# Wider PSUM adds and a new order of the first loads in a windowed matmul

## The chip, the cores and the metric

One core of one Trainium2 chip. The metric is the device time of one execution in microseconds (us). Kernels of one batch ran on the same chip, in turn with the kernel before; the last batch alone shares seven of its eight times of the kernel before with the first, which ran on the same chip. Engines in the profile: PE (matmuls), PEld (weight loads), DVE (VectorE), ACT (ScalarE), POOL (GpSimd), SP (SyncE); a name with q, as in SPq, is that engine's sequencer, which issues the DMAs. The granted clock, for short the clock, is the share of PE's full clock that PE was given in a stretch: 1.00 is all of it.

## The reference

```python
# x: (4, 4096, 4096) float32, w: (4096, 4096) float32, offsets: (4,) int64
for b in range(4):
    o = int(offsets[b])
    results.append(x[b, o:o+64] @ w)
return np.stack(results)          # (4, 64, 4096) float32
```

Four windows of 64 rows make 256 rows, so the work is a 256 x 4096 by 4096 x 4096 product. `w` is 67 MB in float32 and has to be read once; it is by far the most of the traffic.

## The kernel before

The 256 rows are two groups `g` of 128. The 4096 output columns are eight pieces of 512, one PSUM bank each. Pool's DMAs load `w` and cast it to fp16 on the way. Only the first k tile (`w0_32`, 128 rows of `w`) is loaded in float32 on the two hardware queues, one half each, and cast by ScalarE. The windows' offsets are a tiny load of four numbers, which Pool has to read before it can issue the four loads of x.

```python
blocks = [(0,1),(1,1),(2,4),(6,4),(10,4),(14,4),(18,4),(22,3),(25,2),(27,1)]   # first k tile, how many
n_join = 2;  k_tail = 28;  n_fine = 2
tmp = [acc_pool.tile([P, NT], fp32, name=f"tmp{i}") for i in range(4)]
ps  = [psum_pool.tile([P, NT], fp32, name=f"bank{t}") for t in range(8)]       # eight tiles of a bank

nc.sync.dma_start(out=w0_32[:, :NG], in_=w[0:P, :NG])
nc.scalar.dma_start(out=off_t[:], in_=offsets[None, :])
nc.scalar.dma_start(out=w0_32[:, NG:], in_=w[0:P, NG:])
...                                   # cut: casts, second k tile, x loads, weight stream, transposes
def add_out(bank, g, c):
    dst = acc[g][:, c * NT : (c + 1) * NT]
    nc.vector.tensor_add(out=dst, in0=dst, in1=ps[bank][:])

def whole_rows(kts, cols, first):     # stream: block by block, all columns
    for g in range(G):
        for c in cols:
            bank = n_bank % 8; n_bank += 1
            for i, kt in enumerate(kts):
                mm(bank, g, kt, ...)
            if not first: add_out(bank, g, c)
            ...                       # cut: the first block copies in place of adding

def columns(ng, kts):                 # column stages: k outside, four banks per g
    for ki in kts:
        for g in range(G):
            for j in range(n_sub): tail_mm(ki, g, ng, j, ...)     # bank 4 * g + j
    for g in range(G):
        for j in range(0, n_sub, 2):
            add_out(4 * g + j, g, ng * n_sub + j)
            nc.scalar.copy(out=tmp[2 * g + j // 2][:], in_=ps[4 * g + j + 1][:])
    ...                               # cut: the adds from tmp
...                                   # cut: two column stages, stores, k tiles 28 and 29
for h in range(2):                    # the end: two halves of the last two k tiles
    js = range(h * n_sub // 2, (h + 1) * n_sub // 2)
    for ki in range(k_fine, n_k):
        for g in range(G):
            for j in js: tail_mm(ki, g, ng, j, ...)
    for g in range(G):
        for j in js: add_out(4 * g + j, g, ng * n_sub + j)
        store(q[g], g, ...)
```

The last tiles are taken by column stages so that finished halves of the output can be stored while the rest is computed.

Of the kernel before, what the change touches and what calls it, by code (L numbers as in the profile page):

```python
# [10 lines left out]
def kernel(  # L11
# [7 lines left out]
    nc = tc.nc  # L19
    fp32 = mybir.dt.float32  # L20
# [5 lines left out]
    P = 128  # L26
    NT = 512
    NG = N // 2
    n_k = D // P
    n_sub = NG // NT  # L30
    G = B // 2
# [13 lines left out]
    acc_pool = ctx.enter_context(tc.tile_pool(name="acc", bufs=1))  # L45
    psum_pool = ctx.enter_context(tc.tile_pool(name="ps", bufs=1, space=bass.MemoryType.PSUM))

    identity = const_pool.tile([P, P], fp16, name="identity")
    off_t = const_pool.tile([1, B], mybir.dt.int64, name="off_t")
    x16 = [x_pool.tile([P, D], fp16, name=f"xrow{g}") for g in range(G)]  # L50
    xT = [x_pool.tile([P, D], fp16, name=f"xT{g}") for g in range(G)]
    w_one = [w1_pool.tile([P, N], fp16, name=f"w1_{i}") for i in range(2)]
    tmp = [acc_pool.tile([P, NT], fp32, name=f"tmp{i}") for i in range(4)]
    acc = [acc_pool.tile([P, N], fp32, name=f"acc{g}") for g in range(G)]
    ps = [psum_pool.tile([P, NT], fp32, name=f"bank{t}") for t in range(8)]

    ctx.enter_context(tc.manual_schedule())

    w0_32 = acc[1]
    nc.sync.dma_start(out=w0_32[:, :NG], in_=w[0:P, :NG])  # L60
    nc.scalar.dma_start(out=off_t[:], in_=offsets[None, :])
    nc.scalar.dma_start(out=w0_32[:, NG:], in_=w[0:P, NG:])
    nc.scalar.copy(out=w_one[0][:, :NG], in_=w0_32[:, :NG])  # L63
    nc.scalar.copy(out=w_one[0][:, NG:], in_=w0_32[:, NG:])  # L64
    off_i32 = off_t.bitcast(mybir.dt.int32)
# [3 lines left out]
    for b in range(B):  # L69
        g, m = divmod(b, 2)  # L70
# [8 lines left out]
            out=x16[g][m * WIN : (m + 1) * WIN, :],  # L79
            in_=x[b][bass.ds(o, WIN), :],  # L80
# [3 lines left out]
    src = {  # L84
        0: lambda a, e: w_one[0][:, a:e],
        1: lambda a, e: w_one[1][:, a:e],
    }
    free = 0
    for k0, r in blocks[2:]:
        if free < r:  # L90
            t = wc_pool.tile([P, R_MAX * N], fp16, name="wc", tag="wc")
# [4 lines left out]
            out=t[:, base : base + r * N],  # L96
            in_=w[k0 * P : (k0 + r) * P, :].rearrange("(p r) n -> p (r n)", r=r),
# [11 lines left out]
    t = wc_pool.tile([P, R_MAX * N], fp16, name="wc", tag="wc")  # L109
    pos = 0  # L110
    for ng, st in zip(order, (steps, fine_steps)):
        for ki, n, c0, c1 in st:
            wd = c1 - c0
            nc.gpsimd.dma_start(  # L114
                out=t[:, pos : pos + n * wd].rearrange("p (t n) -> p t n", t=n),
                in_=w[ki * P : (ki + n) * P, ng * NG + c0 : ng * NG + c1].rearrange(
                    "(t p) n -> p t n", p=P
                ),
# [7 lines left out]
    def x_cols(g, kt):  # L126
        for k0, r in blocks:
            if k0 <= kt < k0 + r:
                a = k0 * P + kt - k0
                return x16[g][:, a : a + r * (P - 1) + 1 : r]  # L130
        return x16[g][:, kt * P : (kt + 1) * P]

    for g in range(G):
        for t in range(8):
            for i in range(4):
                nc.tensor.matmul(  # L136
                    out=ps[t][:, i * P : (i + 1) * P],
                    lhsT=x_cols(g, 4 * t + i),
                    rhs=identity[:],
                    start=True,  # L140
                    stop=True,
                )
            dst = xT[g][:, t * NT : (t + 1) * NT]
            if t % 2 == 0:
                nc.vector.tensor_copy(out=dst, in_=ps[t][:])  # L145
            else:
                nc.scalar.copy(out=dst, in_=ps[t][:])  # L147

    def mm(bank, g, kt, rhs, start, stop):
        nc.tensor.matmul(  # L150
            out=ps[bank][:],
            lhsT=xT[g][:, kt * P : (kt + 1) * P],
            rhs=rhs,
            start=start,
            stop=stop,
        )

    def add_out(bank, g, c):
        dst = acc[g][:, c * NT : (c + 1) * NT]
        nc.vector.tensor_add(out=dst, in0=dst, in1=ps[bank][:])  # L160

    n_bank = 0

    def whole_rows(kts, cols, first):
        nonlocal n_bank
        for g in range(G):
            for c in cols:
                bank = n_bank % 8
                n_bank += 1
                for i, kt in enumerate(kts):  # L170
                    mm(bank, g, kt, src[kt](c * NT, (c + 1) * NT), i == 0, i == len(kts) - 1)
                if not first:
                    add_out(bank, g, c)
                elif c % 2 == 0:
                    nc.vector.tensor_copy(out=acc[g][:, c * NT : (c + 1) * NT], in_=ps[bank][:])  # L175
                else:
                    nc.scalar.copy(out=acc[g][:, c * NT : (c + 1) * NT], in_=ps[bank][:])  # L177

    whole_rows([0, 1], range(8), True)
    for k0, r in blocks[2:-n_join]:  # L180
        whole_rows(range(k0, k0 + r), range(8), False)
    join = range(blocks[-n_join][0], k_tail)

    def tail_mm(ki, g, ng, j, start, stop):
        c = ng * n_sub + j
        rhs = src[ki](c * NT, (c + 1) * NT) if ki < k_tail else tail[(ki, c)]
        mm(4 * g + j, g, ki, rhs, start, stop)
# [3 lines left out]
    def store(eng, g, c0, c1, cuts=(0, P)):  # L191
        for a, e in zip(cuts, cuts[1:]):
            eng.dma_start(out=out_rows[g * P + a : g * P + e, c0:c1], in_=acc[g][a:e, c0:c1])  # L193

    def columns(ng, kts):
        for ki in kts:
            for g in range(G):
                for j in range(n_sub):
                    tail_mm(ki, g, ng, j, ki == kts[0], ki == kts[-1])
        for g in range(G):  # L200
            for j in range(0, n_sub, 2):
                add_out(4 * g + j, g, ng * n_sub + j)
                nc.scalar.copy(out=tmp[2 * g + j // 2][:], in_=ps[4 * g + j + 1][:])  # L203
        for g in range(G):
            for j in range(1, n_sub, 2):
                c = ng * n_sub + j
                dst = acc[g][:, c * NT : (c + 1) * NT]
                nc.vector.tensor_add(out=dst, in0=dst, in1=tmp[2 * g + j // 2][:])  # L208

    columns(order[1], list(join))  # L210
    ng = order[0]
    columns(ng, list(join) + list(range(k_tail, n_k)))
    for g in range(G):
        store(nc.gpsimd, g, ng * NG, (ng + 1) * NG)

    ng = order[1]
# [6 lines left out]
    for h in range(2):  # L223
# [3 lines that stand above are left out]
                for j in js:  # L227
                    tail_mm(ki, g, ng, j, False, ki == n_k - 1)
        for g in range(G):
            for j in js:  # L230
                add_out(4 * g + j, g, ng * n_sub + j)
            c0 = ng * NG + h * NG // 2
            store(q[g], g, c0, c0 + NG // 2)

# [29 lines left out]
```

## Time and profile before

| what | value |
|---|---|
| time, median of 3 | 182.1 us (182.09 to 182.39) |
| span of the profiled run | 180.2 us |
| PE busy | 127.2 us (71%) in 576 instructions |
| DVE busy | 90.6 us (50%) in 136 instructions |
| ACT, POOL busy | 18.3 and 12.7 us |
| read from and written to memory | 71.30 and 4.19 MB |

Busy shares are averages over stages with different limits: neither PE nor DVE is full.

### The profile page before, as it was taken

To read this page: it belongs to the slowest core of one execution; us is meant where nothing else is said; L and a number is where in the kernel's file an instruction comes from. 1 tells how busy PE (TensorE), PEld (TensorE's weight loads), DVE (VectorE), ACT (ScalarE), POOL (GpSimd) and SP (SyncE) were. 2 spreads that over 40 slices of the span, in tenths; PEclk is the share of its full clock that TensorE was granted. 3 is DMA by queue.
4 is the path that set the end of the run, shared out by engine and by line. 5 is a ranking of instruction groups with operands and counts; after the bars stand their busy time and mean duration, and the time that the engine had idled before them with its cause. 6 is when DMAs were issued, how large, how long until landed. Compare 5 with 4: busy or idle time off the path is not lost.

```text
span 180.2 us, 1537 instructions
## 1 busy us (share of the span) xinstructions
PE 127.2 (71%) x576; PEld 57.0 (32%) x576; DVE 90.6 (50%) x136; ACT 18.3 (10%) x27; POOL 12.7 (7%) x27
## 2 busy tenths in 40 slices
PE   0000789104999499938996599949999999998900
PEld 0000754001344134403442134414444444443400
DVE  0000678100487347833686147725879966409560
ACT  2412556200000000000000000000000004004000
POOL 4600000000000100010001000020007100001100
PEclk9999999855699979996999569987999999999995
DMA  5999989999998899999989999989999999999995
GB/s 186 316 256 216 276 175 204 236 233 226 233 226 189 175 233 233 235 222 233 196 189 211 233 233 218 229 180 213 224 209 215 195 211 213 216 211 208 372 411 209
DMA packets 4152, 40.98 MB, mean 227 GB/s; under 512 B 434, under 2 KB 434, under 8 KB 2226
## 3 DMA queue, kind: packets, MB, share of 16 engines
q0 software_dynamic: 3280, 36.70, 93.4%
q1 hardware_dynamic: 432, 2.10, 3.2%
q10 hardware_dynamic: 434, 2.10, 2.9%
q8 instruction: 4, 0.07, 0.1%
q14 instruction: 2, 0.02, 0.0%
HBM read 71.30 MB, written 4.19 MB: 419 GB/s over the span
## 4 chain that ended last, share of the span: by engine, by line
DMA 58%; PE 30%; issue 3%; DVE 2%; another core or an unknown queue 1%; POOL 1%; POOLq 1%; DVEq 0%
DMA wc<-in_w_dram 58%; PE bank L150 30%; DVE acc L160 2%; POOL wc L114 1%; POOLq L71 1%; POOL xrow L78 0%; DVEq L259 0%; POOL identity masks.py:197 0%; POOLq L78 0%; POOL w L67 0%; POOLq masks.py:199 0%; POOLq L248 0%
## 5 line engine op out<-in xcount | busy, mean ns | idle before, releaser
L150 PE MATMUL bank<-wc,xT 128*128 128x512 f16 x480 | 115.0, 405 | 24.3 <-DMA wc<-in_w_dram 24.3
L160 DVE TENSOR_TENSOR acc<-acc,bank 128x512 f32<-128x512 f32 x112 | 75.2, 687 | 61.5 <-PE bank L150 60.9
L150 PEld LDWEIGHTS <-xT 128*128 128x128 f16 x512 | 52.1, 103 | 93.8 <-DMA wc<-in_w_dram 27.2
L136 PE MATMUL bank<-identity,xrow 128*128 128x128 f16 x64 | 5.3, 258 | 20.0 <-DMA xrow<-in_x_dram 20.0
L203 ACT COPY tmp<-bank 128x512 f32<-128x512 f32 x8 | 4.1, 599 | 127.5 <-PE bank L150 127.5
L145 DVE CAST xT<-bank 128x512 f16<-128x512 f32 x8 | 5.3, 687 | 21.0 <-PE bank L136 20.9
L95 POOL DMA_DIRECT2D wc<-in_w_dram x8 | 4.3, 540 | 108.1 <-PE bank L150 108.1
L136 PEld LDWEIGHTS <-xrow 128*128 128x128 f16 x64 | 5.0, 124 | 20.1 <-issue 20.1
L150 PE MATMUL bank<-w,xT 128*128 128x512 f16 x32 | 7.1, 379 | 0.0
L175 DVE COPY acc<-bank 128x512 f32<-128x512 f32 x8 | 5.4, 688 | 0.9 <-PE bank L150 0.6
L114 POOL DMA_DIRECT2D wc<-in_w_dram x6 | 3.9, 674 | 17.1 <-PE bank L150 17.1
L147 ACT CAST xT<-bank 128x512 f16<-128x512 f32 x8 | 4.4, 593 | 7.1 <-PE bank L136 7.0
L208 DVE TENSOR_TENSOR acc<-acc,tmp 128x512 f32<-128x512 f32 x8 | 5.0, 682 | 0.0
L177 ACT COPY acc<-bank 128x512 f32<-128x512 f32 x8 | 4.7, 586 | 2.1 <-PE bank L150 1.9
L193 POOL DMA_DIRECT2D out_dram<-acc x2 | 1.1, 538 | 26.6 <-DVE acc L208 26.6
L64 ACT CAST w<-acc 128x2048 f16<-128x2048 f32 x1 | 1.9, 1897 | 4.9 <-DMA acc<-in_w_dram 4.9
L78 POOL DMA_DIRECT2D xrow<-in_x_dram x4 | 2.1, 524 | 2.1 <-issue 2.1
L63 ACT CAST w<-acc 128x2048 f16<-128x2048 f32 x1 | 1.9, 1897 | 2.8 <-DMA acc<-in_w_dram 2.8
L63 ACT ACT_TABLE_LOAD x1 | 1.3, 1283 | 1.8 <-PEq L248 1.8
L67 POOL DMA_DIRECT2D w<-in_w_dram x1 | 0.7, 660 | 0.8 <-POOLq L248 0.8
masks.py:199 POOL TENSOR_SCALAR_AFFINE_SELECT identity<-identity 128x128 f16<-128x128 f16 x1 | 0.3, 290 | 0.1
masks.py:197 POOL MEMSET identity<- 128x128 f16 x1 | 0.2, 224 | 0.0
(4 smaller groups left out, 0.4 us busy)
## 6 DMA issues: line engine op xcount, KB each, us to landing
wc<-in_w_dram POOLq DMA_DIRECT2D x5, 4096.0 KB, 42.1
wc<-in_w_dram POOLq DMA_DIRECT2D x4, 1024.0 KB, 24.6
wc<-in_w_dram POOLq DMA_DIRECT2D x1, 3072.0 KB, 37.1
xrow<-in_x_dram POOLq DMA_DIRECT2D x4, 512.0 KB, 14.5
wc<-in_w_dram POOLq DMA_DIRECT2D x1, 2048.0 KB, 26.6
out_dram<-acc POOLq DMA_DIRECT2D x2, 1024.0 KB, 6.3
acc<-in_w_dram SPq DMA_DIRECT2D x1, 1024.0 KB, 5.1
w<-in_w_dram POOLq DMA_DIRECT2D x1, 1024.0 KB, 12.0
```

The source lines that it names most:

```text
L63: nc.scalar.copy(out=w_one[0][:, :NG], in_=w0_32[:, :NG])
L95: nc.gpsimd.dma_start(out=t[:, base : base + r * N], in_=w[k0 * P : (k0 + r) * P, :].rearrange("(p r) n -> p (r n)", r=r),)
L114: nc.gpsimd.dma_start(out=t[:, pos : pos + n * wd].rearrange("p (t n) -> p t n", t=n), in_=w[ki * P : (ki + n) * P, ng * NG + c0 : ng * NG ...
L136: nc.tensor.matmul(out=ps[t][:, i * P : (i + 1) * P], lhsT=x_cols(g, 4 * t + i), rhs=identity[:], start=True, stop=True,)
L145: nc.vector.tensor_copy(out=dst, in_=ps[t][:])
L147: nc.scalar.copy(out=dst, in_=ps[t][:])
L150: nc.tensor.matmul(out=ps[bank][:], lhsT=xT[g][:, kt * P : (kt + 1) * P], rhs=rhs, start=start, stop=stop,)
L160: nc.vector.tensor_add(out=dst, in0=dst, in1=ps[bank][:])
L175: nc.vector.tensor_copy(out=acc[g][:, c * NT : (c + 1) * NT], in_=ps[bank][:])
L177: nc.scalar.copy(out=acc[g][:, c * NT : (c + 1) * NT], in_=ps[bank][:])
L203: nc.scalar.copy(out=tmp[2 * g + j // 2][:], in_=ps[4 * g + j + 1][:])
L208: nc.vector.tensor_add(out=dst, in0=dst, in1=tmp[2 * g + j // 2][:])
```

## The change

The intent: fewer and wider DVE instructions, as each add has a fixed part (0.687 us for 512 columns, but 2.288 and not 2.75 for four times as many in the result), and a start in which ScalarE's queue does not hold its half of the first k tile back behind the offsets. PSUM becomes two tiles of four banks ("quads"), the adds of the stream take four banks at once, those of the stages and of the end two, and ScalarE copies two banks at once into a wider `tmp`. The diff, cut to its core:

```diff
-    tmp = [acc_pool.tile([P, NT], fp32, name=f"tmp{i}") for i in range(4)]
+    tmp = [acc_pool.tile([P, 2 * NT], fp32, name=f"tmp{i}") for i in range(G)]
-    ps = [psum_pool.tile([P, NT], fp32, name=f"bank{t}") for t in range(8)]
+    quads = [psum_pool.tile([P, 4 * NT], fp32, name=f"banks{t}") for t in range(2)]
+    def banks(b, n=1):
+        return quads[b // 4][:, b % 4 * NT : (b % 4 + n) * NT]
     nc.sync.dma_start(out=w0_32[:, :NG], in_=w[0:P, :NG])
-    nc.scalar.dma_start(out=off_t[:], in_=offsets[None, :])
     nc.scalar.dma_start(out=w0_32[:, NG:], in_=w[0:P, NG:])
+    nc.sync.dma_start(out=off_t[:], in_=offsets[None, :])
 ... (ps[b][:] becomes banks(b) everywhere)
     whole_rows:
-            for c in cols:
-                bank = n_bank % 8
+            for c in range(0, 2 * n_sub, 4):
+                b0 = n_quad % 2 * 4
+                for j in range(4): (the four banks' matmuls)
-                    add_out(bank, g, c)
+                    add_out(b0, 4, g, c)
     columns:
-            for j in range(0, n_sub, 2):
-                add_out(4 * g + j, g, ng * n_sub + j)
-                nc.scalar.copy(out=tmp[2 * g + j // 2][:], in_=ps[4 * g + j + 1][:])
+            add_out(4 * g, 2, g, ng * n_sub)
+            nc.scalar.copy(out=tmp[g][:], in_=banks(4 * g + 2, 2))
     the end:
-            for j in js:
-                add_out(4 * g + j, g, ng * n_sub + j)
+            add_out(4 * g + js[0], 2, g, ng * n_sub + js[0])
```

## The prediction

> **What bounds the kernel now.** I read the page first: span 180.2 us for a measured 182.1, so 1.9 us lie outside the span and I carry them over. Then the chain, the rows of the groups, and the timelines of the start and of the last 60 us.
>
> ```profile
> DMA  5999989999998899999989999989999999999995
> ...
> DMA 58%; PE 30%; issue 3%; DVE 2%; another core or an unknown queue 1%; POOL 1%; POOLq 1%; DVEq 0%
> ...
> L150 PE MATMUL bank<-wc,xT 128*128 128x512 f16 x480 | 115.0, 405 | 24.3 <-DMA wc<-in_w_dram 24.3
> L160 DVE TENSOR_TENSOR acc<-acc,bank 128x512 f32<-128x512 f32 x112 | 75.2, 687 | 61.5 <-PE bank L150 60.9
> ...
> L203 ACT COPY tmp<-bank 128x512 f32<-128x512 f32 x8 | 4.1, 599 | 127.5 <-PE bank L150 127.5
> ```
>
> The DMA row is full from about 2 us to the end, and PE's idle time (24.3 us) is all waiting for weights. So the weight stream sets the pace. In the timeline the four-tile blocks begin at 43.1, 62.4, 81.7, 101.1 and 120.4 us: 19.35 us apart, against 15.6 to 16.7 us of matmuls. In that stretch PE has 2.6 to 3.8 us to spare per block and DVE waits for PE. Shorter adds there buy nothing.
>
> The end is different. PE alone, from 120 us:
>
> ```profile
> 120.43 43.22 PE L150 MATMUL bank<-wc,xT 128*128 128x512 f16 x192 [2.61 <-DMA wc<-in_w_dram]
> 164.42 0.82 PE L150 MATMUL bank<-wc,xT 128*128 128x512 f16 x3 [0.77 <-DMA wc<-in_w_dram]
> ```
>
> 192 matmuls run without a gap (192 x 0.216 = 41.5, plus 1.7 while the clock is low), then only 0.77 us are spare. PE delayed by more than 0.77 us in this stretch moves everything after it. The end of the chain and the stores:
>
> ```profile
> 164.42 5.37 PE bank L150 x24
> 169.79 1.57 DVE acc L160 x3
> 171.36 0.19 issue
> 171.55 0.69 DVEq L259
> 172.24 1.79 DVE acc L160 x3
> ```
> ```profile
> 166.15 0.54 POOL L193 DMA_DIRECT2D out_dram<-acc  x1 [25.91 <-DVE acc L208]
> 167.35 0.53 POOL L193 DMA_DIRECT2D out_dram<-acc  x1 [0.66 <-DVE acc L208]
> 169.16 4.87 DVE L160 TENSOR_TENSOR acc<-acc,bank 128x512 f32<-128x512 f32 x8 [2.10 <-PE bank L150]
> ```
>
> The last add ends at 174.03, the last store goes out then and lands 5.2 us later, queued behind other stores. And the start:
>
> ```profile
> 0.86 0.52 ACTq L61 DMA_DIRECT2D off_t<-in_offsets_dram  x1
> 0.87 0.38 SPq L60 DMA_DIRECT2D acc<-in_w_dram  x1
> 1.38 0.66 POOL L67 DMA_DIRECT2D w<-in_w_dram  x1 [0.81 <-POOLq L248]
> 1.41 0.38 ACTq L62 DMA_DIRECT2D acc<-in_w_dram  x1
> ...
> 3.54 0.53 POOL L78 DMA_DIRECT2D xrow<-in_x_dram  x1 [0.92 <-issue]
> ```
>
> The offsets are first on their queue and do not delay Pool: it issues its first x load at 3.54. The queue view for 1.5 to 4.5 us shows how the halves of w0 share the engines:
>
> ```profile
> q1 hardware_dynamic: 101, 0.83, 86.0%
> q10 hardware_dynamic: 2, 0.00, 0.0%
> ```
>
> q1 is sync, q10 scalar. Scalar's half, issued at 1.41, has moved nothing at 4.5 us (its two packets are the offsets); the packet records show it beginning at 4.9, when sync's half is ending, and Pool's first weights at 5.4. The scalar half's cast starts only at 12.7, against 5.94 for sync's half.
>
> **What the Trainium skill says.** "VectorE: DVE Perf Modes", section "The TRN2 errata": an fp32 tensor_tensor takes (N+151)/0.96 ns, a fixed part per instruction. The trace agrees: 691 by the formula, 687 measured. So estimates: 1024 columns 1.22 us, 2048 columns 2.29 us. "PSUM — Partial Sum Buffer", section "PSUM bank collisions raise a hardware error": two engines must keep apart per bank; different banks are free. So the chip needs no wait between banks 0 and 1; any such wait in the new program is the program's own. "DMA: Bandwidth & Descriptors", section "Issuing engines are not separate DMA queues": DMAs of different issuers run on the same engines and interleave. Only half seen here: scalar's half did not interleave with sync's, it followed it. "TensorE: Matmul & The Clock Gate", section "What's actually happening": the clock is granted by windows of 3.4 us. The trace fits: after gaps of 2.6 to 3.8 us PE gets 0.5 for a while, after 0.77 us it does not.
>
> **The change part by part.**
>
> Adds of four banks: 96 adds of 0.687 become 24 of 2.29, DVE busy 66 to 55 us, 11 us less. All beside the weight stream: worth 0. Their price: a quad of four banks is one tile, and the built program's waits show that it is handed over whole. PE may write no bank of a quad before the whole add has ended, where it used to get back bank after bank. With two quads this is free while PE needs over 2.3 us a quad: 16 matmuls are 3.46 us, 12 are 2.59. It is not free where the loop form changes.
>
> (A) From the three-tile block to the first column stage: PE needs the second quad 4 matmuls (0.86 us) after its last one, the add takes 0.1 + 2.29 + 0.1 (handing over, my guess from 0.03 to 0.11 between PE's end and an add's start in the timeline). Stall 2.49 - 0.86 = 1.63 us; before, none.
>
> (B) Between the column stages: the program's waits are now add, then scalar's copy of the other two banks, then PE; before, add and copy used separate banks side by side. A 1024-column copy is 599 + 512 x 0.845 = 1.03 us (slope from 599 ns at 512 and 1897 ns at 2048). For g = 0: the quad ends 0.86 us before the stage's end T; add to T+0.46, copy to T+1.59, PE at T+1.69. For g = 1: copy from T+1.76 to T+2.79, PE at T+2.89, wanted at T+2.55. Stall 1.69 + 0.34 = 2.03 us.
>
> (C) The same from the second column stage to the last steps: 2.03 us.
>
> (D) The last half's matmuls now wait for the first half's add in the same quad. With H the end of the first half: add g0 to H+0.89, PE at H+0.99; add g1 to H+2.09, PE at H+2.19; PE ends at H+3.49 and the last add at H+5.55. Before: H = 169.79, last add 174.03, H+4.24. So 1.3 us more; the adds of two banks themselves save next to nothing (four of 1.22 for eight at a pitch of 0.61).
>
> Sum at the last add: 1.63 + 2.03 + 2.03 - 0.77 + 1.3 = 6.2 us, so 180.25. Then the stores. Before they queued; the last packets left at 178.9, 4.9 us after the last add. Now Pool's stores go out some 4 us later, DMA idles after the weights, and the last 512 KB find an empty queue: about 1.0 us to the first packet (0.87 to 1.87 at the start), 1.3 us at 410 GB/s, some 0.6 us of ramp: 183.1. That is 4.2 us later, about 2 us of the delay having been queueing. The tail costs +4.2.
>
> The start: transposes and first copies now take turns within a quad, about 8 us per g (eight turns of some 0.25 us of matmuls, a cast of 0.69 or 0.59 and two handings over, one turn overlapped) for 3.3 and 2.0 before, but PE stood idle from 32.2 to 43.1 us: hidden. The scalar half moves 0.55 us up; sync's half alone already fills the engines (86% share with the ramp), so this buys 0 to 0.4 us. The offsets are now third among hardware-queue loads. If these are served in turn as above, the second half shares the engines with Pool until about 12 us (12.7 in the trace), the offsets land then, and x goes out 1.2 us later (offsets in at about 2.3, first x load 3.54) plus at least 1 us to its first packet. The 4.2 MB of w0 and w1 are through at about 12.3 us, nothing else is queued, and DMA idles some 2.5 us, which shift the whole stream. If the halves and Pool interleave evenly, the offsets land at about 9.5: 0.3 us. If the offsets need only follow sync's half: -0.2 us. With chances 0.55, 0.25 and 0.20 the mean is +1.4.
>
> **The rivals.** (1) DMA bound throughout, so nothing shows: 182. For it the full DMA row; against it the 0.77 us spare. (2) Cheaper adds release banks earlier and the tail shortens: 181 to 182. Against it the whole-quad waits. (3) Only the tail pays: 186.2. (4) Tail and late offsets: 188.7. (5) A stall of 1.7 to 2 us late on also drops PE's clock for a window, up to 1.7 us more; gaps of 2.6 us did, so I give it one chance in three, +0.5.
>
> **Range and chances.** 182.1 + 4.2 + 1.4 + 0.5 = 188.2; I say 188.0, with 185.3 (tail smaller by 1, no bubble) to 190.8 (bubble and a clock drop). The limit of 2% is 185.7. The tail alone passes it by 0.6, so slower 0.84, within 2% 0.14, faster 0.02.
>
> **What would show it.** Adds of 2.29 and 1.22 us, DVE busy near 79 us. PE in the 192-matmul stretch: gaps of about 1.6 and 2.0 us, released by DVE and by scalar's copy. After the weights a hole in the DMA row of 2 to 3 us, the last add about 6 us later against the weights' landing. The first x load at 13 us (4), 11 or 6.5; the block at 43.1 us later by the bubble. I am wrong if the quads' waits are handed over faster than counted, if stores in an empty queue take much less than 2.9 us, or if PE gains slack before 120 us that I don't see.

## The result, and the profile after

The changed kernel took 189.0 us (median of six runs, 187.5 to 190.0), against 182.1 us (182.0 to 182.4) for the kernel before in the same rounds. The ratio is 1.0376, with a 95% interval from 1.0331 to 1.0422: slower by 3.8%. Ratios here and below are the mean time of one kernel's runs over that of the other's runs in the same rounds, so not quite the ratio of the medians quoted. Executions over 1.5% slower than the fastest of the same kernel are left out of the means. The profiled run of the changed kernel took 188.7 us, with a span of 186.9.

From the page of the changed kernel: the busy times, the granted clock and the DMA share in 40 slices of 4.7 us.

```profile
PE 128.3 (69%) x576; PEld 57.9 (31%) x576; DVE 79.1 (42%) x46; ACT 17.5 (9%) x17; POOL 12.7 (7%) x27
...
PEclk9999999999999999996699889999999999999997
DMA  5978999998999999999999998999999999996696
```

The DVE saving came in full: 90 instructions and 11.5 us less. It bought nothing, for the DMA row has two dents that the row of before does not have: one in the third slice (9 to 14 us) and one three to four slices from the end (168 to 178 us). Loads or stores stand still there, and the two dents belong to the two parts of the change. The adds' groups, split by shape:

```profile
L164 DVE TENSOR_TENSOR acc<-acc,banks 128x2048 f32<-128x2048 f32 x24 | 54.9, 2288 | 46.8 <-PE banks L154 46.8
L164 DVE TENSOR_TENSOR acc<-acc,banks 128x1024 f32<-128x1024 f32 x8 | 9.4, 1217 | 17.0 <-PE banks L154 17.0
```

**The start.** The timeline of the changed kernel's start (start, duration, who, what, and in brackets the idle time before and what ended it):

```profile
0.86 0.40 ACTq L65 DMA_DIRECT2D acc<-in_w_dram  x1
0.87 0.38 SPq L64 DMA_DIRECT2D acc<-in_w_dram  x1
...
1.31 0.32 SPq L66 DMA_DIRECT2D off_t<-in_offsets_dram  x1
...
13.11 0.53 POOL L82 DMA_DIRECT2D xrow<-in_x_dram  x1 [10.49 <-issue]
```

The offsets are issued at 1.31 us, but the packet records show their one packet at 10.94, after both halves of `w0` (done at 9.7 and 10.0). Pool reads the offsets at 11.89 and issues the first x load at 13.11, where it was 3.54. The view of the queues between 1.5 and 4.5 us (packets, MB, share of the 16 engines; q1 is sync's, q10 scalar's) shows that the halves now share the engines:

```profile
q1 hardware_dynamic: 49, 0.40, 51.3%
q10 hardware_dynamic: 40, 0.33, 30.5%
```

By the time that x is issued, everything queued ahead of it has run out. In the table of windows (stretch, its length, then busy time of PE, PEld, DVE, ACT and POOL with their instructions, the clock, the DMA share and GB/s), first the changed kernel, then the kernel before:

```profile
13.00:14.00 1.00, 0.00 (x0) 0.00 (x0) 0.00 (x0) 1.00 (x1) 0.53 (x1) 1.00 0.00 0
173.00:174.50 1.50, 1.39 (x7) 0.58 (x6) 1.45 (x2) 0.18 (x1) 0.54 (x1) 1.00 0.00 0
```

```profile
13.00:14.00 1.00, 0.00 (x0) 0.00 (x0) 0.00 (x0) 1.00 (x1) 0.00 (x0) 1.00 0.94 197
62.00:64.00 2.00, 1.63 (x4) 0.58 (x5) 0.00 (x0) 0.00 (x0) 0.00 (x0) 0.57 1.22 262
173.00:174.50 1.50, 0.00 (x0) 0.00 (x0) 1.03 (x2) 0.00 (x0) 0.00 (x0) 1.00 1.05 429
```

DMA stands still from 13.1 to 14.3 us and is thin around it; the last packet of x ends at 26.6 us instead of 22.7. At 173 us it stands still again: all weights are in, and no store is ready. (The line for 62 us is used below, for the clock.)

**The end.** PE of the changed kernel from the 120-us block on:

```profile
124.70 13.99 PE L154 MATMUL banks<-wc,xT 128*128 128x512 f16 x64 [3.63 <-DMA wc<-in_w_dram]
139.16 11.40 PE L154 MATMUL banks<-wc,xT 128*128 128x512 f16 x52 [0.47 <-DMA wc<-in_w_dram]
152.07 4.48 PE L154 MATMUL banks<-wc,xT 128*128 128x512 f16 x20 [1.52 <-DVE acc L164]
158.04 12.51 PE L154 MATMUL banks<-wc,xT 128*128 128x512 f16 x56 [1.49 <-ACT tmp L208]
172.10 5.61 PE L154 MATMUL banks<-wc,xT 128*128 128x512 f16 x24 [1.55 <-ACT tmp L208]
178.59 0.59 PE L154 MATMUL banks<-wc,xT 128*128 128x512 f16 x2 [0.88 <-DVE acc L164]
179.72 1.46 PE L154 MATMUL banks<-wc,xT 128*128 128x512 f16 x6 [0.54 <-DVE acc L164]
```

Where 192 matmuls ran without a gap before, there is now one wait of 0.47 us for weights and then a gap at each change of stage, and the engine that ends each is named: DVE's wide add, then ScalarE's copy twice, then DVE between the two last halves. After 139.16 PE never again waits for weights. From 139.16 to the end of the first half at 172.10 + 5.61 = 177.71 us are 38.55 us for 52 + 20 + 56 + 24 = 152 matmuls, which at 0.216 us take 32.83: 5.7 us are lost. (The three gaps shown make 4.6. Inside the lines of 158.04 and 172.10 the chain has a second wait of about 0.3 us each, until ScalarE's copy of the other group's quad is done and PE goes on at 159.17 and 173.23. The rest is that the view draws a matmul 0.379 us long, while the next one starts after 0.216.) From there to the end of the last add (183.13) are 5.42 us, where it was 4.24.

### The profile page after: what moved, and what is told of

It is laid out like the page before. It is cut to its first block, busy times and chain, and to the rows that moved or that the text cites. A ratio compares the mean times of both kernels' runs of the same rounds, so it can differ in the third digit from the quotient of the medians.

```text
span 186.9 us, 1367 instructions
## 1 busy us (share of the span) xinstructions
PE 128.3 (69%) x576; PEld 57.9 (31%) x576; DVE 79.1 (42%) x46; ACT 17.5 (9%) x17; POOL 12.7 (7%) x27
## 4 chain that ended last, share of the span: by engine, by line
DMA 50%; PE 31%; DVE 9%; issue 4%; ACT 2%; DVEq 1%; POOLq 0%; SPq 0%; POOL 0%; ACTq 0%
DMA wc<-in_w_dram 40%; PE banks L154 26%; DMA off_t<-in_offsets_dram 6%; PE banks L140 5%; DMA xrow<-in_x_dram 4%; DVE acc L164 3%; DVE xT L149 3%; DVE acc L181 2%; ACT xT L151 1%; ACT tmp L208 1%; DVEq L262 1%; POOLq L75 0%; SPq L64 0%; POOL xrow L82 0%; POOLq L82 0%
## 5 line engine op out<-in xcount | busy, mean ns | idle before, releaser
L154 PE MATMUL banks<-wc,xT 128*128 128x512 f16 x480 | 110.4, 391 | 21.2 <-DMA wc<-in_w_dram 14.3
L164 DVE TENSOR_TENSOR acc<-acc,banks 128x2048 f32<-128x2048 f32 (+1 forms) x32 | 64.3, 2020 | 63.9 <-PE banks L154 63.9
L140 PE MATMUL banks<-identity,xrow 128*128 128x128 f16 x64 | 8.9, 302 | 31.4 <-DMA xrow<-in_x_dram 22.1
L149 DVE CAST xT<-banks 128x512 f16<-128x512 f32 x8 | 5.5, 691 | 34.1 <-PE banks L140 34.1
L208 ACT COPY tmp<-banks 128x1024 f32<-128x1024 f32 x4 | 4.1, 1013 | 117.5 <-DVE acc L164 117.3
L154 PE MATMUL banks<-w,xT 128*128 128x512 f16 x32 | 9.3, 454 | 0.4 <-DVE acc L181 0.4
L181 DVE COPY acc<-banks 128x2048 f32<-128x2048 f32 x2 | 4.6, 2292 | 6.1 <-PE banks L154 6.1
L151 ACT CAST xT<-banks 128x512 f16<-128x512 f32 x8 | 4.7, 586 | 21.5 <-PE banks L140 21.5
L212 DVE TENSOR_TENSOR acc<-acc,tmp 128x1024 f32<-128x1024 f32 x4 | 4.7, 1223 | 0.0
L183 ACT COPY acc<-banks 128x2048 f32<-128x2048 f32 x2 | 3.7, 1866 | 7.0 <-PE banks L154 7.0
```

The costliest lines, as they stand in the source:

```text
L140: nc.tensor.matmul(out=banks(t)[:, i * P : (i + 1) * P], lhsT=x_cols(g, 4 * t + i), rhs=identity[:], start=True, stop=True,)
L149: nc.vector.tensor_copy(out=dst, in_=banks(t))
L151: nc.scalar.copy(out=dst, in_=banks(t))
L154: nc.tensor.matmul(out=banks(bank), lhsT=xT[g][:, kt * P : (kt + 1) * P], rhs=rhs, start=start, stop=stop,)
L164: nc.vector.tensor_add(out=dst, in0=dst, in1=banks(bank, n))
L181: nc.vector.tensor_copy(out=acc[g][:, :NG], in_=banks(b0, 4))
```

## The experiments

The theory: the loss is two separate things. (T1) The offsets behind the half of `w0` let the DMA engines run dry before x is issued, which moves the whole weight stream by about 3 us. (T2) A quad passes from PE to DVE or ScalarE and back as a whole, so PE waits at each change of stage in the part of the kernel where it has no slack. The rivals: the late x itself (transposes done late) in place of the dry queue; the width of an add in place of the tile that is handed over; and a clock that drops after the new stalls. Ten kernels were run, all with correct results. The first four came in one batch (kernel before: 182.03 us), the next four in another (182.13), the last two in a third (182.03).

**1. `start_only`: the kernel before with the new order of loads alone.**

```diff
-    nc.scalar.dma_start(out=off_t[:], in_=offsets[None, :])
     nc.scalar.dma_start(out=w0_32[:, NG:], in_=w[0:P, NG:])
+    nc.sync.dma_start(out=off_t[:], in_=offsets[None, :])
```

> The kernel before with only the new queue order at the start (single banks and single adds kept). Theory S (the start pays by itself): the offsets land at about 11 to 12 us, Pool issues its first x load at about 13 us instead of 3.5, the DMA engines stand idle for 1 to 2 us near 13 us, and the whole weight stream shifts by about 4 us (4.3 in the trace of the changed kernel, of which 3.8 stand at the end of the x loads). PE has single banks, so nothing is added at the end: 186.0, ratio 1.02. Rival T (the tail alone pays, the late offsets are hidden under other loads): 182.1, ratio 1.00.

Measured: 185.0 us (184.9 to 185.2, four runs), ratio 1.0166 (1.0144 to 1.0188). PE's long stretch, with the old adds, is untouched but begins 3.1 us later than the 120.43 of before:

```profile
123.57 43.30 PE L150 MATMUL bank<-wc,xT 128*128 128x512 f16 x192 [3.80 <-DMA wc<-in_w_dram]
```

So the order of loads alone costs 3.0 us, and the whole of it arrives as a shifted weight stream. That is more than the time in which nothing moves, as the queue also runs down and fills again slowly: in the four microseconds from 12 to 16 us the DMA engines moved 90, 0, 131 and 180 GB/s in this trace and 221, 197, 238 and 213 in that of before. The missing 0.47 MB are 2.2 us at the pace of before, an estimate from these figures.

**2. `adds_only`: the changed kernel with the old order of loads.**

```diff
+    nc.scalar.dma_start(out=off_t[:], in_=offsets[None, :])
     nc.scalar.dma_start(out=w0_32[:, NG:], in_=w[0:P, NG:])
-    nc.sync.dma_start(out=off_t[:], in_=offsets[None, :])
```

> The changed kernel with the old queue order at the start (whole quads and wide adds kept). Theory S plus tail: the stalls of PE between the stages stay (1.5 to 2 us each, released by the wide add or by scalar's copy), the last add moves by 5 to 6 us against the landing of the weights, about 2.4 us of that are absorbed where stores used to queue: 184.5, or 186.2 if the block at 120 us starts at half clock; ratio 1.013 to 1.022. Rival (start alone pays): 182.1. If the two parts add, this ratio and that of start_only sum to the changed kernel's 1.038.

Measured: 185.9 us (184.6 to 186.8, four runs), ratio 1.0187 (1.0134 to 1.024). Gaps of 1.52, 1.49, 1.55, 0.88 and 0.54 us stand in the same places as in the changed kernel. The two parts add: 1.66% and 1.87% make 3.53%, and 3.76% (3.31 to 4.22) was measured for both. In microseconds 182.1 + 3.0 + 3.8 = 188.9. The runs are uneven, by 2.2 us; that is taken up below.

**3. `weights_ahead`: `start_only`, but Pool issues the first block of four weight tiles before it reads the offsets.** It keeps x late and gives the DMA engines something to do.

```diff
+    t0 = wc_pool.tile([P, R_MAX * N], fp16, name="wc", tag="wc")
+    k0, r = blocks[2]
+    nc.gpsimd.dma_start(
+        out=t0[:, : r * N],
+        in_=w[k0 * P : (k0 + r) * P, :].rearrange("(p r) n -> p (r n)", r=r),
+    )
     for b in range(B):       # values_load of the offsets and x loads, unchanged
 ...
-    for k0, r in blocks[2:]:
+    for k0, r in blocks[3:]:
```

> start_only with the first four-tile block of weights issued by Pool ahead of the x loads, so that the DMA engines have 8 MB of work while Pool waits for the offsets. Theory (the hole in the DMA row is the cost, not the late x as such): no hole, x lands near 42 us, PE starts its blocks 11 us later but catches up 4 us per block before 120 us: 182.2, ratio 1.00. Rival (the late x costs because PE loses its lead, or because x loads by themselves run slowly): 184 to 187.

Measured: 182.3 us (182.2 to 182.3), ratio 1.0015 (0.9995 to 1.0034). Its PE timeline, the first transposes and the long stretch:

```profile
37.82 3.57 PE L144 MATMUL bank<-identity,xrow 128*128 128x128 f16 x32 [37.82 <-DMA xrow<-in_x_dram]
...
120.99 43.30 PE L158 MATMUL bank<-wc,xT 128*128 128x512 f16 x192 [3.63 <-DMA wc<-in_w_dram]
```

Here x comes far later than in `start_only`, PE begins its first matmul at 37.8 us, and yet the block of 120 us is reached at 121.0, 0.6 us later than before, and at most 0.3% of the time is lost. The late x is not the cost; the dry queue is.

**4. `offsets_first`: the kernel before, sync's queue with the offsets first and then its half, scalar's queue with its half at once.** This gives the change what it wanted, an early second half, without late offsets.

```diff
+    nc.sync.dma_start(out=off_t[:], in_=offsets[None, :])
     nc.sync.dma_start(out=w0_32[:, :NG], in_=w[0:P, :NG])
-    nc.scalar.dma_start(out=off_t[:], in_=offsets[None, :])
```

> The kernel before with scalar's queue beginning with its half of w0 as in the change, but with the offsets in front of sync's half instead of behind it. Theory: it is the place of the offsets that costs, so first x load back at about 3.5 us, no hole in the DMA row, 182.1 plus or minus 0.4, ratio 1.00. Rival: the two halves running at once disturb the start themselves (slower ramp, weights landing later): 183 to 185. The halves should interleave, both landing near 10 us.

Measured: 182.1 us (182.0 to 182.2), ratio 1.0004 (0.9985 to 1.0024). The time is as expected, but the halves did not interleave as I had expected. The queues between 1.5 and 4.5 us:

```profile
q10 hardware_dynamic: 101, 0.83, 86.7%
q1 hardware_dynamic: 2, 0.00, 0.0%
```

It is the picture of before with the parts exchanged: scalar's half, issued at 0.86 us, goes alone, and sync's half, issued at 1.27, moves its first packet at 4.84. So in these runs the halves share the engines only where they are issued in the same instant, as in the changed kernel. Two things go together here, though: wherever the second half came 0.4 to 0.5 us later, it also stood behind the offsets on its own queue, and no run separates the delay from that place. And starting scalar's half earlier gains nothing: one half alone already fills the engines.

**5. `pairs`: old order of loads, four PSUM tiles of two banks, all adds and copies over two banks.**

```diff
-    ps = [psum_pool.tile([P, NT], fp32, name=f"bank{t}") for t in range(8)]
+    pairs = [psum_pool.tile([P, 2 * NT], fp32, name=f"banks{t}") for t in range(4)]
 ... whole_rows:
-            for c in cols:
-                bank = n_bank % 8
+            for c in range(0, 2 * n_sub, 2):
+                b0 = n_quad % 4 * 2
+                for j in range(2): (the two banks' matmuls)
-                    add_out(bank, g, c)
+                    add_out(b0, 2, g, c)
```

> The old queue order at the start; PSUM as four tiles of two banks, and adds and copies over two banks everywhere, in the stream too. Theory (PE waits because a four-bank tile is handed over whole): with pairs the wait at the change from the three-tile block to the column stage falls from 1.5 us to about 0.1 (two banks back 1.4 us after their last matmul, wanted after 0.86 to 1.3), the two between the column stages from 1.5 plus 0.4 to about 0.4 each, and the one between the halves of the last steps vanishes, since the halves use different pairs. Sum below 1 us, of which 0.8 is hidden: 182.0 to 182.6, and runs as even as those of the kernel before. Rival (wider adds are slow as such, or fewer of them leave DVE late): half of the loss of adds_only stays, 183.5 to 184.

Measured: 182.2 us (181.8 to 182.6), ratio 0.9998 (0.9983 to 1.0013). PE's last stretch has no gap at all:

```profile
120.55 52.19 PE L154 MATMUL banks<-wc,xT 128*128 128x512 f16 x224 [3.73 <-DMA wc<-in_w_dram]
```

The stages' adds and copies are as wide here as in `adds_only`, so there only the tiles differ. With twice as many tiles of half the size, an add or copy of one pair lies beside PE's work on the other three, and the end stage's first half uses other tiles than the second. DVE is down to 82.9 us in 72 instructions, at no cost and no gain.

**6. `quads_four_adds`: `adds_only` with each add of the stream cut into four adds of one bank on the same quad.**

```diff
-                    add_out(b0, 4, g, c)
+                    for j in range(4):
+                        add_out(b0 + j, 1, g, c + j)
```

> adds_only with the wide add of the stream cut into four adds of one bank, on the same four-bank tiles. Theory (the handing over of the tile costs, not the width of the add): nothing is won back, the first wait of PE is now 4 adds long, 0.687 + 3 x 0.6 = 2.5 us instead of 2.3, plus 0.1 us per quad in the three-tile block: 185 to 187, as adds_only or up to 0.5 above it. Rival (the width costs): 182 to 183.5.

Measured: three runs from 184.9 to 187.1 us, a fourth of 188.4; ratio 1.0214 (1.0156 to 1.0272). PE's gap at the first change of stage:

```profile
150.44 4.48 PE L154 MATMUL banks<-wc,xT 128*128 128x512 f16 x20 [1.71 <-DVE acc L164]
```

The adds are as narrow as before the change, and the gap is 1.71 us, not less than the 1.52 of the wide ones. By an estimate, a wait for the first bank alone would have been next to nothing: an add of one bank takes 0.69 us, and PE wants the quad four matmuls, 0.86 us, after it has filled it. So what PE waits for here is the quad, handed over whole, whatever the width of the adds that empty it.

**7. `offsets_between`: the kernel before with all three loads on the sync queue: half, offsets, half.**

```diff
-    nc.scalar.dma_start(out=off_t[:], in_=offsets[None, :])
-    nc.scalar.dma_start(out=w0_32[:, NG:], in_=w[0:P, NG:])
+    nc.sync.dma_start(out=off_t[:], in_=offsets[None, :])
+    nc.sync.dma_start(out=w0_32[:, NG:], in_=w[0:P, NG:])
```

> The kernel before with sync's queue alone at the start: first half of w0, offsets, second half of w0. Theory (offsets land when what stands ahead of them on the hardware queues is through; the hole opens only if that is later than some 10 us): offsets land at about 5.7, first x load at about 7, no hole, 182.1 plus or minus 0.3. Rival (any place of the offsets behind a large load opens the hole): first x load at 12 to 13 us, 185.

Measured: 182.0 us (181.9 to 182.3), ratio 0.9998 (0.9982 to 1.0013). The first x load:

```profile
6.65 0.53 POOL L78 DMA_DIRECT2D xrow<-in_x_dram  x1 [4.02 <-issue]
```

The offsets follow one half here and have one half behind them. They are through at 4.87 us, x goes out 3.1 us later than before, and nothing is lost, as there is still a half of `w0` and a tile of Pool's to move. This is the case in which the offsets follow only sync's half; the change did not get it because its two halves took turns.

**8. `adds_warm`: `adds_only` with 20 useless matmuls ahead of the 120-us block (k tile 18), to keep the clock up.** They write a free quad that is overwritten afterwards, so the result stays correct.

```diff
     for k0, r in blocks[2:-n_join]:
+        if k0 == 18:
+            for i in range(20):
+                mm(n_quad % 2 * 4, 0, 0, w_one[0][:, :NT], True, True)
         whole_rows(range(k0, k0 + r))
```

> adds_only with 20 matmuls of no use into the free quad ahead of the four-tile block at k = 18, in the 3.6 to 5.3 us that PE waits there, so that PE's clock is not lowered when that block starts (the result stays right: the block's first matmul overwrites). Theory (the uneven runs of adds_only, 184.6 to 186.8, come from how long the clock is low after 120 us, since from there on PE has no slack): the spread shrinks to below 1 us and the time falls to the fast end, 184.4 to 184.9. Rival (the spread comes from elsewhere, such as the stores or the DMA engines): spread and median as adds_only, 185.5 to 186.

Measured: 184.8 us (184.5 to 185.6, five runs), ratio 1.0155 (1.0133 to 1.0177); the spread falls from 2.2 to 1.1 us. The windows (columns as above) of 121 to 125 us and of the stretch with the stalls, first `adds_only`, then `adds_warm`:

```profile
121.00:125.00 4.00, 4.00 (x11) 1.38 (x10) 0.00 (x0) 0.00 (x0) 0.00 (x0) 0.50 0.97 209
...
134.00:172.00 38.00, 33.23 (x152) 14.68 (x151) 22.57 (x14) 4.05 (x4) 4.24 (x7) 1.00 0.93 188
```

```profile
121.00:125.00 4.00, 4.00 (x21) 1.79 (x19) 0.05 (x1) 0.00 (x0) 0.00 (x0) 1.00 1.06 227
...
134.00:172.00 38.00, 33.23 (x151) 14.55 (x150) 20.96 (x14) 4.05 (x4) 5.00 (x8) 1.00 0.96 202
```

Two things follow. Much of the unevenness comes from the start of the 120-us block: after a wait for weights (5.3 us in the profiled run of `adds_only`) the clock is 0.50 for some microseconds, and 116 matmuls take 28.17 us there against 25.33 when kept warm. This run alone does not settle what that is worth, as its interval overlaps that of `adds_only`; run 10 does. The kernel before meets a low clock there too (0.50 from 120.5 to 123.7 us, 1.00 after that; in `adds_only` it is still 0.58 from 123.7 to 127.0), but its wait for weights at 164 us takes it up: `offsets_between` had a clock of 1.00 at that place (120.5 to 124.5 us), and its last block of matmuls still began at 164.40 us, against 164.42 before. With the quads there is no slack left to do so. And the new stalls of 1.5 us do not lower the clock: it is 1.00 over 134 to 172 us in both kernels, which both have them.

**9. `after_again`: the changed kernel, once more,** to have it on the chip of the next one.

> The changed kernel once more, for a second trace. If the two parts simply add: 187.5 to 190, median 188.9 (182.1 + 3.0 from start_only + 3.8 from adds_only). In the first trace the blocks of weights landed 3.2 to 4.3 us later, in start_only 2.9 to 3.1; if that excess is chance, this trace shows 3 to 3.5; if the whole-quad casts slow the x loads, it shows about 4 again.

Measured: 189.4 and 188.5 us, ratio 1.0379 (1.0341 to 1.0418), as at first. In this trace the 120-us block begins at 123.35 us, 2.9 later than before, with a clock of about 0.5 for its first microseconds; in the first trace it began 4.3 later, but at full clock. The two offset each other there. So the shift of the stream varies by over a microsecond from run to run.

**10. `after_warm`: the changed kernel with the 20 useless matmuls of `adds_warm`.**

> The changed kernel with the 20 matmuls of no use ahead of the block at k = 18, as in adds_warm. Theory (uneven runs come from the clock after 120 us): spread of the changed kernel (187.5 to 190.0) shrinks to about 1 us and the time falls to its fast end, 187.5 to 188. Rival: 188.5 to 189.5 with the same spread.

Measured: 187.5 us (187.0 to 188.3, four runs), ratio 1.0293 (1.0264 to 1.0321). Its interval lies clear below that of `after_again`: the clock at the 120-us block is worth 1.4 us to the changed kernel, and the spread falls from 2.5 (six runs) to 1.3 us. Even so it stays 2.9% behind.

No version beat the kernel before. `pairs`, `offsets_first` and `offsets_between` equal it. There is little left to win: 75.5 MB at the stream's pace (a block of 8.39 MB read per 19.35 us, 433 GB/s) would be 174 us, an estimate, and DMA of the kernel before is busy from 1.9 to 178.9 us, so some 3 us are not yet used.

## Why the prediction was right

It said 188.0 us (185.3 to 190.8), slower; 189.0 was measured. The mechanism of both parts was right, while one term was 1.6 us too small and two were together 0.9 too large. That the total came within 1.0 us is in part luck: these errors in part cancel, and the +1.4 of the start was a mean of three cases, none of which occurred. Rival (4), tail and late offsets, had named 188.7, the nearest to what came.

- **Wide adds are worth nothing by themselves.** Right: DVE's busy time fell to 79.1 us, as said, the adds took 2.288 and 1.217 us, and `pairs`, which saves two thirds of that time without the waits, is level with the kernel before.
- **Steps A, B and C, whole quads handed over.** Right, and nearly to the number: 1.63 + 2.03 + 2.03 = 5.69 us were predicted, 5.7 are lost in the changed kernel's trace. `quads_four_adds` and `pairs` show that the tile's size makes them, not the adds' width: the first for step A, the second, with equal widths, for B and C.
- **Step D.** 1.3 us predicted; 5.42 - 4.24 = 1.18 measured.
- **The stores take up some of it.** About 2 us were predicted to vanish, as stores no longer queue. In `adds_only` the last add ends at 181.21 us, 7.2 later than before, and that run took 186.78 us, 4.75 more than the 182.03 of before: 2.4 us vanish. The last packets left 2.5 us after the last add in the changed kernel, where 2.9 was estimated; the hole in the DMA row before the stores was 1.6 us in that trace and 3.7 in `after_again`, where 2 to 3 was said. So the tail cost +3.8 (`adds_only`, median), where +4.2 was said.
- **The start.** This term was mis-sized: +1.4 stood in the sum as a mean of three cases, and 3.0 was measured (`start_only`). No case occurred as it was drawn. The halves shared the engines, as in the second case, but the offsets landed as late as in the first (10.94 us), since their packet went only when both halves were through. The chain from there was right: x was issued 1.2 us after the offsets were read and moved its first packet 1.2 us later, with nothing else queued. The first case's 2.5 us was close to the measured 3.0.
- **The slower transposes are hidden.** Right: PE took from 22.14 to 40.25 us for those of both groups, 9 us each where about 8 was said, and began the first four-tile block at 50.32, on a wait for DVE; at the next block (66.68) it already waited 2.39 us for weights again.
- **The clock.** The +0.5 for a drop after the late stalls was wrong: stalls of 1.5 us leave it at 1.00. There is a clock effect, elsewhere: the old low clock at the 120-us block, harmless before, is now on the path. The tail's sum had it inside already, as it set out from the timeline of before with its 1.7 us; `adds_warm` has 1.1 us of it back, within its noise, and `after_warm` 1.4.

With the measured terms, 182.1 + 3.8 + 3.0 = 188.9. The start was 1.6 too small, the tail 0.4 and the clock 0.5 too large.

What stays open: why two halves issued in the same instant share the engines while those issued 0.4 to 0.5 us apart follow each other, and whether the time or the place behind the offsets decides that; and why the offsets' packet came a microsecond after sync's half was through.

## What to carry to other kernels

Before widening an instruction, ask what tile it frees and who waits for that tile: where a loop changed its form, PE got a large tile back only when all of it was done, and tiles half as large (here four pairs in place of two quads) gave adds of two banks everywhere without the wait. A tiny load on which other loads depend belongs ahead of the bulk, or between two pieces of it, so that there is always something else queued while its answer is awaited. In a kernel that is bound by its loads, look for the stretch in which the other engines have no slack, mostly the end, and count a change's waits there first.

## What the Trainium skill lacked or had wrong

- "DMA: Bandwidth & Descriptors", "Issuing engines are not separate DMA queues": it says that DMAs of different issuers interleave. Here the two halves of `w0`, 1 MB each, did so only when issued in the same instant (51% and 31% of the engines). Issued 0.41 or 0.54 us apart, with the offsets ahead of the second on its queue, the second moved none of its data until 4.8 to 4.9 us, when the first was ending (shares 81 to 87% against 0.0% over the traces). Which of the two matters is not settled.
- "TensorE: Matmul & The Clock Gate", "HAM oscillation — how this bites in real kernels": it gives as the rule that gaps of PE should not be over about 3.4 us. Here a gap of 2.57 us (59.80 to 62.37 us of the kernel before) was enough: the clock was 0.57 between 62 and 64 us, as the line shown above says. And a gap of 3.63 us (before 124.70 us in the changed kernel's first trace) left it at 1.00 from 124.7 to 128.7 us. So the length of a gap alone does not decide here. Gaps of 1.5 us did not lower it (1.00 over 134 to 172 us).
- "DMA: Bandwidth & Descriptors", "Latency and other measured facts": it gives about 1 us to the first byte of a Pool DMA. The x load behind an empty queue agrees (issued at 13.11, first packet at 14.3 us). Pool's first weight load, issued at 1.38 us while the hardware queues were full, moved its first packet only at 5.4 us, and at 5.5 in the changed kernel, where both halves were still under way; no page tells of such a wait, and its cause is not settled here.
- None of the pages read says that a PSUM tile of several banks is handed over as a whole by the program's own waits, however few of its banks an instruction touches. It cost about 1.5 us at each change of stage, with adds of four banks and, in `quads_four_adds`, of one.
